# ScalarE's table loaded behind a copy of a constant, and the compressed attention of a decoder block in one stacked product for three

## The chip, the core and the metric

One core of a Trainium2 chip runs the whole kernel. The metric is the device time of one execution in microseconds (us); less is better. The engines are named as in the profile: PE is TensorE's matmul, PEld its weight load, DVE is VectorE, ACT is ScalarE, POOL is GpSimd, SP is SyncE, which here only issues DMAs.

## What is computed

One layer of a decoder trunk for 256 rows of 2048 columns, float32. The part that the change touches is the sparse attention with compressed keys and values:

```python
hn = rms_norm(h, ln_gain[l])
z = split_columns(hn @ w_in[l] + b_in[l])
y_a = rglru_branch(...) * silu(z['lru_gate'])
k_c = rms_norm(compress(z['nsa_k_cmp'], ...), nsa_k_gain[l])   # 15 compressed keys for each of 2 heads
v_c = compress(z['nsa_v_cmp'], cmp_pos[l, 1], cmp_w1[l, 1], cmp_w2[l, 1])
y_b = nsa_branch(q_b, k_c, v_c, k_s, v_s, k_w, v_w, g_b) * silu(z['nsa_gate'])
#   in it: o_c = p_c @ v_c, and out = g0 * o_c + g1 * o_s + g2 * o_w
y_c = fox_branch(...) * silu(z['fox_gate'])
merged = mg0 * (y_a @ w_branch[0]) + mg1 * (y_b @ w_branch[1]) + mg2 * (y_c @ w_branch[2])
h = h + merged @ w_out[l]
h = h + sigmoid(h @ w_ple_gate[l]) * rms_norm(p[l] @ w_ple[l], ple_gain[l])
```

`compress` is `silu(windows @ w1) @ w2` over 15 windows of 32 rows.

## The kernel before

Precision is kept by splitting each float32 operand into two float32r parts, `hi` (ACT copies it, rounding) and `lo` (DVE subtracts `hi` from the source). A product is then three matmuls, hi*hi, hi*lo, lo*hi, into the same PSUM bank (`mm3`).

The kernel is a stream of weights. `plan()` cuts all weight matrices into 385 pieces of at most 128 x 1024; each is loaded into one of four `raw` tiles by a DMA that SP issues (`issue`), split by ACT and DVE into `wh` and `wl` (`cut`, up to three pieces ahead, in a ring of four buffers each), and used by PE (`by_rows`, `by_cols`) into the PSUM banks `main0` to `main3`. Beside the stream runs the rest, as Python generators (`Side`): each step of a task is emitted between two pieces of the stream, in an order that a rough clock of the engines (`Clock`) decides when the program is built. On the chip each engine works through its own list in that order. The tasks use the PSUM banks `bank0` to `bank3`, and tiles of the pools `k1`, `k2`, `k4`, whose number in use `ROOMS` bounds; at most three tasks are under way.

Three places matter here.

- **The start** (`block_kernel`, "loads and constants"). ACT issues the DMAs of the small vectors `vec` and of the constants `cst`; SP issues by turns a tile of x (`xT`) and the first weights (`raw`). PE multiplies constants meanwhile (`WARM` = 8 products of 128 x 128 float32, each two passes in the trace). The first instruction of ACT with arithmetic is the split of x times its gain (`hn_first`, tile `hnh`); ahead of it stands ACT's table load. The first chunk is `cmp`, eight pieces of two 128-row tiles, 24 matmuls each.
- **`cmp_end`**: the hidden values `hid` of the compressed keys and values, their second product with `w2`, and the compressed values of each head as two tiles of 15 rows, `vch` and `vcl`.
- **`nsa_task(g, pr, t)`**, eight of them: two heads of a group and one row tile. It makes the scores, `soft` gives the probabilities `pc` (16 columns, compressed) and `p` (selected and window), DVE scales them with the gates, PE turns them (transposes against `ident`), and ACT and DVE split what comes out. The output is a sum in one bank: 6 matmuls (t = 0) or 12 (t = 1) of `pth`, `ptl` with the values `vv`, and then one `mm3` of 15 rows, `pch`, `pcl` with `vch`, `vcl`:

```python
        mm3(out, vch[:, g, :], vcl[:, g, :], pch[:NCMP].rearrange("p a q -> p (a q)"),
            pcl[:NCMP].rearrange("p a q -> p (a q)"), False, True)
```

Of the kernel before, what the change touches and what calls it, by code (L numbers as in the profile page):

```python
# [13 lines left out]
OP = mybir.AluOpType  # L14
# [14 lines left out]
HID = 256  # L29
KT = D // P  # L30
# [10 lines left out]
# The small vectors, one column of 128 rows each.  # L41
# [8 lines left out]
# Constants of the shapes alone.  # L50
# [9 lines left out]
# Columns of the input projection whose products come out with rows on partitions, by chunk.  # L60
# [15 lines left out]
def plan():  # L76
    """The order of the weights: pieces of products, with what each needs and starts."""
# [63 lines left out]
class Clock:  # L141
    """Estimates, in ns, of when each engine is through with what was emitted for it: an instruction
    starts once its engine is free and the last uses of its operands that matter to it are over."""
# [6 lines left out]
    def add(self, which, cost, out, ins, late=0.0):  # L150
# [3 lines left out]
        for ap, writes in regions:  # L154
            free = list(ap.ap)[1:]
            lo = ap.offset
            hi = lo + sum(s * (n - 1) for s, n in free)
            name = ap.tensor.name
            # Two engines take turns at a bank of PSUM, whatever they do there.
            bank = name.startswith(("bank", "main"))  # L160
            if bank:
                lo, hi = 0, 1 << 30
            spans.append((name, lo, hi, writes))
            for l, h, t, w, e in self.uses.get(name, ()):
                if (writes or w or bank and e != which) and l <= hi and lo <= h:
                    start = max(start, t + (0.0 if e == which else 60.0))
# [14 lines left out]
class Metered:  # L181
    """An engine whose work is added to the clock."""
# [37 lines left out]
class Side:  # L220
    """Work beside the stream of weights, cut into steps that are dealt out along it."""
# [17 lines left out]
    def tick(self, hurry=False):  # L239
        """One step of every task that is under way, as long as the engines keep up."""  # L240
# [17 lines left out]
    def take(self, n=1):  # L258
        """n banks that are through with what was last in them."""
# [11 lines left out]
    def settle(self):  # L271
        """Until a product that reads what was emitted so far needn't wait for it."""
# [5 lines left out]
    def room(self, **need):  # L278
        """Room for a task's tiles."""
# [14 lines left out]
def block_kernel(ctx: ExitStack, tc: tile.TileContext, io):  # L294
# [44 lines left out]
    def splits(*parts):  # L339
        """Each source (times a scale) as the exact sum of two float32r tensors."""  # L340
# [16 lines left out]
    # ------------------------------------------------------------------ the stream of weights  # L357
# [4 lines left out]
    def issue(h, k=0, nk=None):  # L362
        """Loads a half's rows of 128, or nk of them from the k-th."""
# [20 lines left out]
    def by_rows(h, x):  # L384
        """Rows on partitions: two main banks, one of each row tile, gather the chunk's products."""
# [14 lines left out]
    def by_cols(h, x):  # L400
        """Columns on partitions: the chunk's column tiles in halves of main banks."""
# [14 lines left out]
    def banks_of(h):  # L416
        """The main banks of by_cols, each with its (first column tile, number of them)."""
# [7 lines left out]
    # ------------------------------------------------------------------ loads and constants  # L425
# [7 lines left out]

    A.dma_start(vec, io["vec"])
    for i in range(4):
# [8 lines left out]
    # The causal mask of a tile, with none before and after.  # L444
# [9 lines left out]
    half_n = cp.tile([P, 8], F32, name="half_n")  # L454
    ones = cp.tile([P, P], F32, name="ones")
    V.memset(half_n, -0.5)
    V.memset(ones, 1.0)
    # Products of constants until the first weights are in: the array's clock rises with use.
# [3 lines left out]
    def rsqrt(out, ss, n):  # L462
        """out = (ss / n + EPS) ** -0.5"""
# [4 lines left out]
    def softplus(out, x, n):  # L468
        """out = max(x, 0) + log1p(exp(-|x|)), with log1p(u) = 2 atanh(u / (2 + u))"""
# [14 lines left out]
    def squares(x, acc, first):  # L484
        """acc += x^2, of two tiles"""
# [7 lines left out]
    def row_scales(name, acc):  # L493
        """(mean square of each of the 256 columns + EPS) ** -0.5, the same on all partitions."""
# [18 lines left out]
    # ------------------------------------------------------------------ operands kept on chip  # L513
# [9 lines left out]
    vch, vcl = (cp.tile([NCMP, 2, P], R32, name=n) for n in ("vch", "vcl"))  # L523
# [3 lines left out]
    def hn_first(i, ks=range(2)):  # L527
        """Two tiles of x times its gain, as operands; the rows' scales come later."""
# [9 lines left out]
    def hn_again(i):  # L538
        """The same with the rows' scales."""
# [14 lines left out]
    # ---- p @ w_ple, normed, with its gain halved for the last gate  # L554
# [28 lines left out]
    # ---- gates: half of z (1 + tanh(z / 2)) is z sigmoid(z)  # L583
# [11 lines left out]
    # ---- RG-LRU, two tiles of 128 channels at a time  # L595
    def lru_task(i):
# [43 lines left out]
        # 1 - a^2 = tanh(-log a) (1 + a^2)  # L640
# [12 lines left out]
    # ---- keys and values of the sparse attention  # L653
    def unscaled(banks, dst, name, k0):
        """A chunk of the products without the rows' scales."""
# [9 lines left out]
    def cmp_task(banks):  # L665
        """The windows of 32 rows, with their positions added: 15 columns for each row and head."""
# [19 lines left out]
    def cmp_end():  # L686
# [6 lines left out]
        # The products with both parts of each block, added and turned.  # L693
# [7 lines left out]
        V.tensor_tensor(hid, hp, sg, op=OP.mult)  # L701
        yield from side.settle()
        for q in range(2):
            T.matmul(banks[b][:30, 128:256], hid[:, q, :], w2[:, 0, q, :], start=q == 0, stop=q == 1)
        for g in range(2):
            for q in range(2):
                T.matmul(banks[b][:NCMP, 256 + g * P:256 + (g + 1) * P], hid[:, 2 + q, g * NCMP:(g + 1) * NCMP],
                         w2[:, 1, q, :], start=q == 0, stop=q == 1)
        yield True
        split(vch, vcl, banks[b][:NCMP, 256:512].rearrange("p (g d) -> p g d", g=2))  # L710
# [14 lines left out]
    def norm_rows(z, n, dst):  # L725
        """dst(t) = z's groups of 128 columns, each row of a group normed."""
# [15 lines left out]
    def kk_task(z):  # L742
        # Of each head: window keys of row tiles 1 and 0, compressed keys, selected keys of tiles 0 and 1.
# [21 lines left out]
    # ---- sparse attention of a pair of heads and one row tile  # L765
    def nsa_task(g, pr, t):
# [5 lines left out]
        yield from side.room(k1=2, k4=1)  # L772
# [9 lines left out]
        pc = sml([P, 2, 16], name="pc")  # L782
        p = mid([P, 2, 2, n * P], name="prob")

        def soft(a, sc):
            """exp(score - maximum) and their sums: compressed, selected, window."""
# [30 lines left out]
        for a in range(2):  # L817
            V.tensor_scalar(pc[:, a, :], pc[:, a, :], s[:, a, 0:1], None, op0=OP.mult)
# [16 lines left out]
        yield from side.room(k1=2)  # L835
        b, = yield from side.take()
        for a in range(2):
            T.transpose(banks[b][:16, 256 + a * P:256 + (a + 1) * P], pc[:, a, :], ident)
        yield True
        pch, pcl = one([16, 2, P], R32, name="pch"), one([16, 2, P], R32, name="pcl")  # L840
        split(pch, pcl, banks[b][:16, 256:512].rearrange("p (a q) -> p a q", a=2))
        yield from side.settle()
        out = banks[b][:, :S]
        for i in range(2 * n):
# [5 lines left out]
        mm3(out, vch[:, g, :], vcl[:, g, :], pch[:NCMP].rearrange("p a q -> p (a q)"),  # L850
            pcl[:NCMP].rearrange("p a q -> p (a q)"), False, True)
# [6 lines left out]
    # ---- forgetting attention  # L858
    def forget_task():
# [10 lines left out]
        # lf holds softplus(-f) = -log f: the running sum is minus the cumulative log forget gate.  # L870
# [10 lines left out]
    def fox_task(h):  # L881
# [42 lines left out]
        # Key tile 0 of both row tiles, then key tile 1 of the second.  # L924
# [17 lines left out]
    # ---- branch outputs as operands  # L942
# [24 lines left out]
    def split_turned(name, dst, src, j, scale=None):  # L967
        """Columns 512 j .. of src, turned and split into dst."""
# [15 lines left out]
    # ------------------------------------------------------------------ the ends of chunks  # L984
# [49 lines left out]
    def read_by(name, gen):  # L1034
        """A task that reads the chunk's main banks."""
# [30 lines left out]
    def proj_chunk(h, out):  # L1066
        """merged += projection (1 + tanh): twice the gated sum, halved when it is split."""
# [33 lines left out]
    def before(h):  # L1101
        """What the end of a chunk asks for, loaded while its products are formed."""
# [202 lines left out]
```

## Time and profile before

| | |
|---|---|
| timed runs | 1108.59, 1110.47, 1111.84 us; median 1110.47 |
| profiled execution | span 1108.5 us from its first to its last instruction; no other time of it is listed, and the shortest timed run is 0.1 us above this span |
| PE busy | 99% of the span, 6123 matmul passes |
| DVE, ACT, POOL busy | 65%, 53%, 5% |
| chain that ended last | PE 97% |
| DMA | 199 GB/s on average |

Busy shares count the time in which an instruction of the engine was under way; matmuls overlap, so the pace of PE is read from the start of one product to the start of the next. "Idle before" is the time in which an engine had nothing under way ahead of an instruction, with what ended it.

### The profile page before, as it was taken

Reading aid. Unit: us, or ns where it says so; the run is one execution under the profiler, and the core shown is the slowest. Engines: PE = TensorE matmul, PEld = TensorE weight load, DVE = VectorE, ACT = ScalarE, POOL = GpSimd, SP = SyncE. Lnnn points to the kernel's source line nnn. Section 1 sums busy time; section 2 is a strip of 40 time slices with the busy share of each in tenths; the row PEclk is TensorE's granted clock in tenths of the full one; section 3 lists DMA queues with packets and bytes.
Section 4 is the critical chain, followed back from the end, with each engine's and each line's share of the span. In section 5 each row is a group of like instructions: output and inputs, shape, how many; then the busy total and the mean of one; then the engine's idle time right before and its main releaser. Section 6 shows DMA issues by size and latency. Waiting matters only on the chain.

```text
span 1108.5 us, 16051 instructions
## 1 busy us (share of the span) xinstructions
PE 1098.8 (99%) x6123; PEld 957.4 (86%) x6123; DVE 725.9 (65%) x1108; ACT 588.2 (53%) x869; POOL 51.0 (5%) x70
## 2 busy tenths in 40 slices
PE   8999999999999999999999999999999999999998
PEld 8999998789988888888888888889888888888888
DVE  7679878877674765676776755554665565555554
ACT  7456786587654655454644544454554444444442
POOL 0100000010000000011010000000000100000000
PEclk9999999999999999999999999999999999999999
DMA  8656658756464554567557566766575775655773
GB/s 303 219 186 187 212 179 267 257 182 195 156 208 148 172 170 138 172 203 212 175 177 218 167 196 202 218 193 217 171 216 195 237 279 195 208 190 180 226 244 101
DMA packets 63293, 220.88 MB, mean 199 GB/s; under 512 B 7400, under 2 KB 8304, under 8 KB 63216
## 3 DMA queue, kind: packets, MB, share of 16 engines
q1 hardware_dynamic: 58176, 203.71, 55.6%
q0 software_dynamic: 4752, 15.76, 5.5%
q8 instruction: 48, 0.79, 0.3%
q10 hardware_dynamic: 288, 0.39, 0.1%
q14 instruction: 29, 0.24, 0.1%
HBM read 215.62 MB, written 4.20 MB: 198 GB/s over the span
## 4 chain that ended last, share of the span: by engine, by line
PE 97%; DMA 1%; DVE 1%; ACT 1%; issue 0%; DVEq 0%; ACTq 0%
PE main L191 90%; PE bank L191 7%; DMA raw<-in_w 1%; DVE wl L191 1%; ACT wh L191 0%; DMA k_xT<-in_xT 0%; ACT L191 0%; DVE k_fin L191 0%; DVE k_z L191 0%; ACT k_lru L191 0%; ACT k_hnh L191 0%; ACT k_fin L191 0%; DVEq L191 0%; ACTq L191 0%
## 5 line engine op out<-in xcount | busy, mean ns | idle before, releaser
L191 DVE TENSOR_TENSOR wl<-raw,wh 128x1024 fp32r<-128x1024 f32 (+3 forms) x385 | 463.8, 1211 | 320.2 <-ACT wh L191 319.1
L191 ACT ACTIVATE wh<-raw 128x1024 fp32r<-128x1024 f32 (+3 forms) x385 | 401.2, 1048 | 376.2 <-PE main L191 297.3
L191 PE MATMUL main<-wh,k_hnh 128*128 128x512 f32 (+1 forms) x736 | 285.0, 387 | 0.9 <-ACT wh L191 0.9
L191 PE MATMUL main<-wl,k_hnh 128*128 128x512 f32 (+1 forms) x736 | 281.3, 382 | 1.2 <-DVE wl L191 1.1
L191 PE MATMUL main<-wh,k_hnl 128*128 128x512 f32 (+1 forms) x736 | 281.0, 382 | 0.0
L191 PE MATMUL main<-k_hnh,wh 128*128 128x256 f32 x576 | 164.7, 286 | 1.5 <-ACT wh L191 1.5
L191 PE MATMUL main<-k_hnh,wl 128*128 128x256 f32 x576 | 164.1, 285 | 0.2 <-DVE wl L191 0.2
L191 PE MATMUL main<-k_hnl,wh 128*128 128x256 f32 x576 | 164.0, 285 | 0.0
L191 PEld LDWEIGHTS main<-wl,k_hnh 128*128 128x128 f32 x736 | 138.5, 188 | 26.7 <-DVE wl L191 2.6
L191 PEld LDWEIGHTS main<-wh,k_hnl 128*128 128x128 f32 x736 | 138.2, 188 | 26.7
L191 PEld LDWEIGHTS main<-wh,k_hnh 128*128 128x128 f32 x736 | 138.4, 188 | 26.3 <-ACT wh L191 1.2
L191 PEld LDWEIGHTS main<-k_hnh,wh 128*128 128x128 f32 x576 | 111.3, 193 | 2.0 <-ACT wh L191 1.8
L191 PEld LDWEIGHTS main<-k_hnh,wl 128*128 128x128 f32 x576 | 111.3, 193 | 0.5 <-DVE wl L191 0.4
L191 PEld LDWEIGHTS main<-k_hnl,wh 128*128 128x128 f32 x576 | 111.4, 193 | 0.1
L191 PE MATMUL main<-wh,k_yh 128*128 128x512 f32 x192 | 75.3, 392 | 0.0
L191 PE MATMUL main<-wh,k_yl 128*128 128x512 f32 x192 | 74.9, 390 | 0.0
L191 PE MATMUL main<-wl,k_yh 128*128 128x512 f32 x192 | 74.9, 390 | 0.0
L191 PE MATMUL main<-wh,k_hth 128*128 128x512 f32 (+1 forms) x160 | 55.7, 348 | 0.0
L191 PE MATMUL main<-wh,k_htl 128*128 128x512 f32 (+1 forms) x160 | 55.6, 347 | 0.0
L191 PE MATMUL main<-wl,k_hth 128*128 128x512 f32 (+1 forms) x160 | 55.5, 347 | 0.0
L191 PE MATMUL main<-wh,k_mth 128*128 128x512 f32 x128 | 50.7, 396 | 0.0
L191 PE MATMUL main<-wh,k_mtl 128*128 128x512 f32 x128 | 50.0, 391 | 0.0
(253 smaller groups left out, 1173.9 us busy)
## 6 DMA issues: line engine op xcount, KB each, us to landing
raw<-in_w SPq DMA_DIRECT2D x371, 512.0 KB, 4.1
bias<-in_b_in POOLq DMA_DIRECT2D x21, 256.0 KB, 4.3
raw<-in_w SPq DMA_DIRECT2D x8, 408.0 KB, 5.4
e_dram<-k_e POOLq DMA_DIRECT2D x4, 512.0 KB, 7.0
k_xc<-in_x POOLq DMA_DIRECT2D x4, 512.0 KB, 8.7
k_xT<-in_xT SPq DMA_DIRECT2D x7, 256.0 KB, 5.8
k_ec<-e_dram POOLq DMA_DIRECT2D x3, 512.0 KB, 7.8
out<-k_fin SPq DMA_DIRECT2D x6, 256.0 KB, 2.2
```

The costliest lines, as they stand in the source:

```text
L191: r = call(out, *args, **kw)
```

## The change

At the start, a copy of eight columns of a constant (`half_n`, set by DVE) is put on ACT right behind the DMA of `vec`, so that the table load stands ahead of this copy, and the DMA of `cst` behind it. PE gets 11 products of constants in place of 8. In `cmp_end` the hidden values of the compressed values are laid out three times, 32 columns apart, in a zeroed tile `hid3`, so that the second product gives 80 rows that hold the 15 values three times; `vc3` keeps them as hi, hi, lo. In `nsa_task` the compressed probabilities are laid out three times in a zeroed tile `pc3`, turned into 80 rows, and `pct` keeps them as hi, lo, hi. One matmul over 80 rows gives the sum of the three products. The tile `pc3` is taken with `qh` and `ql`, so that a task asks for three `k1` tiles at its start and one later, where it asked for two and two.

```diff
+NC3 = 80
...
-    vch, vcl = (cp.tile([NCMP, 2, P], R32, name=n) for n in ("vch", "vcl"))
+    vc3 = cp.tile([NC3, 2, P], R32, name="vc3")
...
+    half_n = cp.tile([P, 8], F32, name="half_n")
+    ones = cp.tile([P, P], F32, name="ones")
+    V.memset(half_n, -0.5)
+    V.memset(ones, 1.0)
     A.dma_start(vec, io["vec"])
+    A.activation(sml([P, 8], name="tbl"), half_n, AF.Copy)
...
     A.dma_start(cst, io["cst"])
...
 def cmp_end():
+        hid3 = two([P, 2, 2, 96], name="hid3")
+        G.memset(hid3, 0.0)
+        for i in range(3):
+            V.tensor_copy(hid3[:, :, :, 32 * i:32 * i + NCMP], hid[:, 2:, :].rearrange("p q (g i) -> p q g i", g=2))
...
-                T.matmul(banks[b][:NCMP, 256 + g * P:256 + (g + 1) * P], hid[:, 2 + q, g * NCMP:(g + 1) * NCMP],
+                T.matmul(banks[b][:NC3, 256 + g * P:256 + (g + 1) * P], hid3[:, q, g, :NC3],
                          w2[:, 1, q, :], start=q == 0, stop=q == 1)
-        split(vch, vcl, banks[b][:NCMP, 256:512].rearrange("p (g d) -> p g d", g=2))
+        v3 = banks[b][:NC3, 256:512].rearrange("p (g d) -> p g d", g=2)
+        A.activation(vc3, v3, AF.Copy)
+        V.tensor_tensor(vc3[64:], v3[64:], f(vc3[64:]), op=OP.subtract)
...
 def nsa_task(g, pr, t):
-        yield from side.room(k1=2, k4=1)
+        yield from side.room(k1=3, k4=1)
...
-        pc = sml([P, 2, 16], name="pc")
+        pc, pc3 = sml([P, 2, 16], name="pc"), one([P, 2, 96], name="pc3")
+        G.memset(pc3, 0.0)
...
-            V.tensor_scalar(pc[:, a, :], pc[:, a, :], s[:, a, 0:1], None, op0=OP.mult)
+            V.tensor_scalar(pc3[:, a, :].rearrange("p (i c) -> p i c", i=3)[:, :, :16],
+                            pc[:, a, None, :].to_broadcast([P, 3, 16]), s[:, a, 0:1], None, op0=OP.mult)
...
-        yield from side.room(k1=2)
+        yield from side.room(k1=1)
         b, = yield from side.take()
         for a in range(2):
-            T.transpose(banks[b][:16, 256 + a * P:256 + (a + 1) * P], pc[:, a, :], ident)
+            T.transpose(banks[b][:NC3, 256 + a * P:256 + (a + 1) * P], pc3[:, a, :NC3], ident)
         yield True
-        pch, pcl = one([16, 2, P], R32, name="pch"), one([16, 2, P], R32, name="pcl")
-        split(pch, pcl, banks[b][:16, 256:512].rearrange("p (a q) -> p a q", a=2))
+        pct = one([NC3, 2, P], R32, name="pct")
+        src = banks[b][:NC3, 256:512].rearrange("p (a q) -> p a q", a=2)
+        A.activation(pct, src, AF.Copy)
+        V.tensor_tensor(pct[32:64], src[32:64], f(pct[32:64]), op=OP.subtract)
...
-        mm3(out, vch[:, g, :], vcl[:, g, :], pch[:NCMP].rearrange("p a q -> p (a q)"),
-            pcl[:NCMP].rearrange("p a q -> p (a q)"), False, True)
+        T.matmul(out, vc3[:, g, :], pct.rearrange("p a q -> p (a q)"), start=False, stop=True)
...
-WARM = 8
+WARM = 11
```

The change also moves instructions, since the builder's clock and the rooms see other tasks. Three places are shown; L191 and L192 are the line of the same helper, through which all instructions go. On ACT, the first rows before:

```order
L191 DMA vec<-in_vec 128x184
L191 DMA cst<-in_cst 128x574
L191 ACT_TABLE_LOAD
L191 ACTIVATE k_hnh_125<-k_xT_91,vec 128x256
L191 ACTIVATE wh_142<-raw_97 128x512
```

and with the change:

```order
L192 DMA vec<-in_vec 128x184
L192 ACT_TABLE_LOAD
L192 ACTIVATE sp_tbl_100<-half_n 128x8
L192 DMA cst<-in_cst 128x574
L192 ACTIVATE k_hnh_130<-k_xT_91,vec 128x256
L192 ACTIVATE wh_146<-raw_103 128x512
```

The load stands ahead of the copy of the constant, and the DMA of `cst` has gone behind both.

On PE, the end of the first `nsa_task` before (`pth`, `ptl`, `pch`, `pcl` are the probabilities, `vv`, `vch`, `vcl` the values):

```order
L191 MATMUL bank_90<-k_pth_3583,k_vv_2106 128x256 x2
L191 MATMUL bank_90<-k_ptl_3584,k_vv_2106 128x256
L191 MATMUL bank_90<-k_pth_3583,k_vv_2106 128x256
L191 MATMUL bank_90<-k_pch_3739,vch 128x256
L191 MATMUL bank_90<-k_pcl_3740,vch 128x256
L191 MATMUL bank_90<-k_pch_3739,vcl 128x256
L191 MATMUL main_85<-wh_3709,k_hnh_125 128x512
```

and with the change:

```order
L192 MATMUL bank_90<-k_pth_3565,k_vv_2110 128x256 x2
L192 MATMUL bank_90<-k_ptl_3566,k_vv_2110 128x256
L192 MATMUL bank_90<-k_pth_3565,k_vv_2110 128x256
L192 MATMUL bank_90<-k_pct_3609,vc_142 128x256
L192 MATMUL main_83<-wh_3614,k_yh_3464 128x512
```

Three products have become one, and the task now ends one part of a chunk earlier, ahead of a product with `yh` rather than `hnh`.

On POOL, the rows from the second product of the compressed keys to the end of the eight tasks before (`bias` is the bias of the next chunk, loaded into a single buffer):

```order
L191 TENSOR_TENSOR sp_kcs_2767<-sp_kcs_2767,half_n 30x1
L191 DMA c_dram<-k_csum_2772 8x256
L191 TENSOR_TENSOR sp_nss_2878<-sp_nss_2878,half_n 128x8
L191 DMA bias_3477<-in_b_in 128x512
L191 DMA bias_3755<-in_b_in 128x512
L191 DMA bias_4124<-in_b_in 128x512
L191 DMA bias_4502<-in_b_in 128x512
```

and part of them with the change:

```order
L192 TENSOR_TENSOR sp_nss_2867<-sp_nss_2867,half_n 128x8
L192 MEMSET k_pc_455_3290 128x192
L192 MEMSET k_pc_460_3302 128x192
L192 DMA bias_3474<-in_b_in 128x512
L192 MEMSET k_pc_503_3586 128x192
L192 DMA bias_3793<-in_b_in 128x512
L192 MEMSET k_pc_555_3896 128x192
L192 MEMSET k_pc_565_3952 128x192
L192 DMA bias_4163<-in_b_in 128x512
```

The zeroing of `pc3` for each task stands on POOL between the DMAs of the biases.

## Rows read from the trace of the kernel before

**Rows 1.** The profile's page: the span, busy time of the engines, the clock granted to TensorE in 40 equal slices (tenths), and the shares of the chain that ended last.

```profile
span 1108.5 us, 16051 instructions
PE 1098.8 (99%) x6123; PEld 957.4 (86%) x6123; DVE 725.9 (65%) x1108; ACT 588.2 (53%) x869; POOL 51.0 (5%) x70
PEclk9999999999999999999999999999999999999999
PE 97%; DMA 1%; DVE 1%; ACT 1%; issue 0%; DVEq 0%; ACTq 0%
```

**Rows 2.** What PE waited for in the whole execution, the two longest in total: us in total, times, the longest.

```profile
PE main L191 <- ACT wh L191: 2.5, 2, 1.5
PE main L191 <- DVE wl L191: 1.4, 3, 0.7
```

**Rows 3.** Timeline of PE at the end of the first `nsa_task`, 335.7 to 337.9 us: start, duration (us), engine, operation, out<-in, shapes.

```profile
336.52 0.28 PE L191 MATMUL bank<-k_pth,k_vv 128*128 128x256 f32 x1
336.73 0.38 PE L191 MATMUL bank<-k_pch,vch 15*128 15x256 f32 x1
336.95 0.28 PE L191 MATMUL bank<-k_pcl,vch 15*128 15x256 f32 x1
337.07 0.27 PE L191 MATMUL bank<-k_pch,vcl 15*128 15x256 f32 x1
337.28 0.50 PE L191 MATMUL main<-wh,k_hnh 128*128 128x512 f32 x1
337.62 0.40 PE L191 MATMUL main<-wl,k_hnh 128*128 128x512 f32 x1
337.85 0.39 PE L191 MATMUL main<-wh,k_hnl 128*128 128x512 f32 x1
```

**Rows 4.** The group of the first of the three products: line, operands, shapes and count, then busy us and mean ns of one, and idle time before.

```profile
L191 PE MATMUL bank<-k_pch,vch 15*128 15x256 f32 x8 | 3.1, 382 | 0.0
```

**Rows 5.** Timeline of PE at the eight passes over 60 rows in `cmp_end`, same columns as rows 3.

```profile
228.46 0.39 PE L191 MATMUL main<-wh,k_hnl 128*128 128x512 f32 x1
228.78 1.07 PE L191 MATMUL bank<-cst,k_hs 60*128 60x30 f32 x8
229.78 0.50 PE L191 MATMUL main<-wh,k_hnh 128*128 128x512 f32 x1
230.12 0.40 PE L191 MATMUL main<-wl,k_hnh 128*128 128x512 f32 x1
```

**Rows 6.** Timeline of PE at two transposes to 16 columns, and at two to 128 columns.

```profile
330.26 0.38 PE L191 MATMUL bank<-cst,sp_pc 128*16 128x128 f32 x2
...
330.71 0.40 PE L191 MATMUL main<-wl,k_hnh 128*128 128x512 f32 x1
...
372.89 0.38 PE L191 MATMUL bank<-cst,k_qn 128*128 128x128 f32 x2
...
373.34 0.39 PE L191 MATMUL main<-wl,k_hnh 128*128 128x512 f32 x1
```

**Rows 7.** Timeline of ACT at the start, with the idle time ahead and what ended it.

```profile
4.01 1.28 ACT L191 ACT_TABLE_LOAD   x1 [4.01 <-DMA k_xT<-in_xT]
5.31 0.51 ACT L191 ACTIVATE k_hnh<-k_xT,vec 128x256 fp32r<-128x256 f32 x1
9.28 1.06 ACT L191 ACTIVATE wh<-raw 128x1024 fp32r<-128x1024 f32 x1 [0.34 <-DMA raw<-in_w]
```

**Rows 8.** Timeline of PE and DVE at the start (the constants' products, the first piece's, and the weights of the second piece).

```profile
1.09 3.76 PE L191 MATMUL bank<-ones 128*128 128x128 f32 x16 [1.09 <-DVE ones L191]
6.39 0.39 PE L191 MATMUL main<-k_hnh,wh 128*128 128x256 f32 x1 [1.54 <-ACT wh L191]
10.36 1.23 DVE L191 TENSOR_TENSOR wl<-raw,wh 128x1024 fp32r<-128x1024 f32 x1 [0.91 <-ACT wh L191]
11.41 0.34 PE L191 MATMUL main<-k_hnl,wh 128*128 128x256 f32 x1
11.64 0.39 PE L191 MATMUL main<-k_hnh,wl 128*128 128x256 f32 x1
```

**Rows 9.** Busy time by stretch of the start: start:end, length, then busy us (and instructions) of PE, PEld, DVE, ACT, POOL, TensorE's granted clock, DMA share, GB/s.

```profile
4.70:8.10 3.40, 1.64 (x11) 1.29 (x11) 2.17 (x4) 2.65 (x6) 0.00 (x0) 1.00 1.02 370
8.10:11.50 3.40, 3.40 (x18) 3.40 (x17) 2.02 (x3) 2.96 (x6) 0.00 (x0) 0.50 1.04 399
11.50:14.90 3.40, 3.40 (x29) 3.29 (x29) 3.15 (x7) 3.40 (x6) 0.00 (x0) 1.00 1.03 406
```

**Rows 10.** The same view of the stretch in which the eight tasks stand, with the columns of rows 9.

```profile
285.00:465.00 180.00, 180.00 (x921) 151.26 (x920) 115.28 (x277) 98.69 (x208) 2.15 (x4) 1.00 0.49 164
```

**Rows 11.** Who waited for whom from 225 to 465 us: us in total, times, the longest.

```profile
DVE wl L191 <- ACT wh L191: 63.1, 44, 3.7
ACT wh L191 <- PE main L191: 41.4, 27, 2.6
```

**Rows 12.** Groups on POOL and DVE that are nearest to the new memsets and copies: count, busy us, mean ns (or, in the last, least, median and greatest ns).

```profile
L191 POOL TENSOR_TENSOR sp_nss<-sp_nss,half_n 128x8 f32<-128x8 f32 x7 | 15.7, 2244 | 235.6 <-DVE sp_nss L191 179.8 <-ACT wh L191 40.8 <-DVE sp_fs L191 14.9
L1298 POOL MEMSET const-float32-1.0<- 128x1 f32 x1 | 0.1, 95 | 0.0
L191 DVE MEMSET ones<- 128x128 f32 x1 | 0.2, 165 | 0.0
L191 DVE TENSOR_SCALAR sp_pc<-sp_pc,sp_sm x16: 225/232/235, 294.5 to 446.4; 128x16 f32<-128x16 f32 x16
```

More of the change, by code (lines that the diff above doesn't have):

```diff
@@ L453, in block_kernel @@
     c_dram = dp.tile([8, S], F32, name="c_dram")
[L454 to L457, printed above, removed]
     for _ in range(WARM):
```

## The prediction

> **What bounds the kernel now.** First the page: PE is busy 99% of the span, its clock is granted in full in nearly every slice, and 97% of the chain that ended last is PE [rows 1]. DVE and ACT, the next two, are busy 65% and 53%. A busy share alone could hide slow matmuls, so I looked next at what PE waited for: 2.5 us for ACT and 1.4 us for DVE are the two longest totals of 1108 us [rows 2]. So PE works through its list almost without a stop, and the time is the sum of the paces of its products. That gives the rule for the rest: what shortens PE's list by a microsecond is worth a microsecond, and what another engine gains or loses is worth nothing as long as PE does not wait for it. Then I read the two places of the change in the timeline: the end of a sparse attention task, and the first 15 us.
>
> **The stacked product.** In the timeline a product of 256 columns is followed by the next after 0.12 us (336.95 to 337.07), one of 512 columns after 0.23 us (337.62 to 337.85). At the three products of 15 rows the pace is broken [rows 3]: from the last `pth` product at 336.52 it takes 0.21, 0.22, 0.12 and 0.21 us to the next starts, and 0.34 us from the first `main` product to the second. Together 336.52 to 337.62 is 1.10 us, where the `pth` product and one `main` product would take 0.12 + 0.23 = 0.35 us. So the three cost 0.75 us: 3 x 0.12 for their columns, and 0.39 us in four breaks of about 0.1 us, two where the rows go from 128 to 15 and two where they go back. There are eight such places [rows 4].
>
> What one product over 80 rows costs is not in the trace; nothing in it has between 60 and 128 rows. The bounds are these. If it runs like the products of 128 rows around it, it costs 0.12 us, and a task saves 0.63 us, eight tasks 5.0 us. If the breaks stay, it costs 0.12 + 0.39 = 0.51 us, a task saves 0.24 us, and eight save 1.9 us. The row with most rows below 128 is the group over 60: it has the same breaks, 0.32 in place of 0.23 us going in (228.46 to 228.78) and 0.34 in place of 0.23 us coming out (229.78 to 230.12) [rows 5]. So the break does not grow or shrink with the rows, from 15 to 60: it looks like a change of the array's arrangement that a product makes or doesn't. By count, 80 is nearer to 60 than to 128; but 15 and 60 rows both fit into half of the array and 80 do not, and I take that as the dividing line: 5.0 us, chance about three in four.
>
> The Trainium skill, page "TensorEngine Tiling (Array Packing)", sections Tiling Modes and Key Properties, says that the array runs with 128, 64 or 32 rows to a tile, and that a change of mode drains the engine. By that rule 80 rows need the same mode as 128, the breaks go, and the sum would be 5.0 us. Against it, the same skill's page "TensorE: Matmul & The Clock Gate", section Why this matters for your kernels, says that a single product over 32 rows takes the same time as one over 128; by that alone only two products of 0.12 us fall away per task, 1.9 us in all. The trace speaks against the second as it stands, since 15 rows cost 0.25 us a product with the breaks and 0.12 us without.
>
> **What is added beside it.** The transposes of the probabilities now give 80 columns for 16. Two to 16 columns take 330.26 to 330.71, two to 128 columns 372.89 to 373.34 [rows 6]: 0.45 us both, to the second `main` product. So 80 cost the same: 0, with 8 x 0.02 us as the bound. In `cmp_end` eight passes over 128 rows give 80 columns for 15: 0 by the same rows. ACT's split keeps its number of columns, and so does DVE's subtraction. DVE gets 16 scalings of 48 columns for 16 columns, each 0.23 us before [rows 12], at most about 0.05 us more each, under 1 us in all, and three small copies of some 0.25 us once. DVE was busy 115 of 180 us in the stretch of the tasks [rows 10], and ACT waited 41.4 us there for PE to give weight buffers back [rows 11]. That idle time is the cover, and I cost these at nothing.
>
> POOL gets nine memsets. POOL was busy 2 of the 180 us [rows 10]. A memset of one column takes 0.095 us there, one of 128 columns on DVE 0.165 us; the farthest row, a power of 8 columns on POOL, takes 2.2 us [rows 12]. I take 0.3 us for 192 columns, the memsets being nearer than a power. Each stands in POOL's queue between the DMAs of the biases, and DVE's scaling waits for it; behind that scaling, on DVE, stand the next `wl` pieces, and for those PE waits. The cover is the store of up to three cut pieces, each 12 products of 0.23 us = 2.8 us of PE, so about 8 us. At 0.3 us nothing comes through.
>
> The order of the tasks moves too, but PE's products in it are the same, and the pace of a `main` product does not depend on where a group of 128 rows is put in. I cost it at nothing; without the cover just named, each piece cut late would cost its lateness.
>
> **The start.** ACT sits until the first tile of x lands at 4.01, loads the table for 1.28 us, and starts the first split at 5.31 [rows 7]. PE is through with the constants at 4.85, sits 1.54 us, and starts at 6.39 [rows 8]. With the load done earlier the split can start at about 4.0 and the first product up to 1.28 us earlier, at 5.1 or, if the weights land after x, later. The constants took 3.76 us for 8, 0.47 us each [rows 8], so 11 end at 1.09 + 11 x 0.47 = 6.3 at the latest, and PE starts the real work between 0.1 and 1.28 us earlier. Does that reach the end? No, by the next row: the second piece of weights lands at 9.28, after an idle ACT [rows 7], with the DMA engines full (share 1.02 to 1.04) [rows 9]. ACT and DVE cut it to 11.59, and PE starts on `wl` at 11.64 [rows 8]. The DMAs ahead of that piece are the same in bytes; `cst` only moves among them. So PE arrives earlier at 11.64 and waits there: gain 0, bounded above by the whole load, 1.28 us.
>
> It can cost instead. After the idle 1.54 us the granted clock was 0.50 from 8.1 to 11.5, the lower level of 1.2 GHz, and full again after 3.4 us of work without a pause [rows 9]. At the half clock PE spread its first 26 products up to 11.41, and lost nothing, since the next had to wait anyway. With the change PE has these 26 done by about 9 at 0.12 us each, and then waits some 2.5 us until 11.6. If a stretch at half clock follows this pause as it followed the other, it falls on products that nothing covers: 18 products against 29 in an equal stretch at the full clock [rows 9], 11 x 0.12 = 1.3 us. Between 0 and 1.3 us I take +0.7 us, the middle, since nothing in the rows says where such a stretch would begin.
>
> **The sum.** Against the profiled execution's span, which lies 0.1 us below the shortest run: 1108.5 - 5.0 + 0.7 = 1104.2 us. The median of the runs shown lies 2.0 us above that span, so as a median: 1110.5 - 4.3 = **1106.2 us**.
>
> **Rivals.**
> 1. *The breaks stay with 80 rows.* For it: 80 is nearer to 60 than to 128. Then 1110.5 - 1.9 + 0.7 = 1109.3 us. This is also the case in which the change does not do what its three-for-one promises beyond two products less, and the same time follows from the second page named above.
> 2. *The start gains as well.* If the second piece lands earlier because `cst` no longer stands ahead of the first weights, the load's 1.28 us come through: 1110.5 - 5.0 - 1.3 = 1104.2 us. Against it stands the full DMA share.
> 3. *Slower: the memset of `pc3` holds DVE.* From about 8 us beyond its due time, the store of cut pieces is empty, and every further microsecond is paid in each of eight tasks. For a net loss of 3.3 us it has to cost 3.3 + 4.3 = 7.6 us, about 1 us past the cover per task: 1114 us. Only a memset of 9 us would do it, four times the longest POOL row.
>
> **How the numbers follow.** Chances: forecast 0.70, rival 1 0.18, rival 2 0.08, rival 3 0.04. About 0.3%, 3.3 us, is what a measurement of this kernel can tell from no change; the three runs before already spread over 3.2 us. Faster by more means under 1107.1 us. The forecast's own range is 1103.5 to 1108.0 (start 0 to +1.3, and the spread of a median by about 1 us); about 0.8 of it lies under 1107.1, so 0.56. Rival 2 adds 0.07, rival 1 0.02: faster 0.65. Slower is rival 3, 0.04. The rest, 0.31, is within 0.3%. For eight in ten I reach up to rival 1, 1110.0, and down to 1103.0, rival 2 less the spread.
>
> **What would show it.** Right: at the ends of the tasks one product over 80 rows starts 0.12 us after the last `pth`, and the next `main` 0.12 us after it. Wrong: starts 0.2 us apart there. At the start: the table load ends before x lands, the first product starts at 5.3 to 6.3, PE waits again until about 11.6, and the granted clock may be half somewhere after that; the first `wl` of the second piece well before 11.6 would speak for rival 2. PE waits from 285 to 465 us, of which there were none, with DVE's scaling into `pc3` behind a POOL memset, would speak for rival 3.

## The result, and the profile after

The changed kernel takes 1104.10 us (median of five runs, 1103.58 to 1106.32) where the kernel before takes 1110.41 (five runs, 1108.59 to 1111.84): a ratio of 0.9948 with an interval of 0.9936 to 0.9959, 0.52% or 5.8 us less (the ratio is of the means; the medians lie 6.3 us apart). The profiled execution has a span of 1101.6 us and a time of its own of 1103.76. The forecast was 1106.2 us, 2.1 us too high; the measured median lies inside the forecast's own range of 1103.5 to 1108.0.

The page of the changed kernel, its span, busy times, granted clock and chain, answers to [rows 1]:

```profile
span 1101.6 us, 16062 instructions
PE 1092.9 (99%) x6113; PEld 954.5 (87%) x6113; DVE 728.5 (66%) x1111; ACT 587.4 (53%) x870; POOL 52.3 (5%) x79
PEclk9999999999999999999999999999999999999999
PE 96%; DVE 1%; ACT 1%; DMA 1%; issue 0%; SPq 0%; DVEq 0%; ACTq 0%
```

PE is busy 5.9 us less and is still the bound. It has ten passes fewer: 16 less at the eight tasks, 6 more from three more constants in two passes each. The waits of PE over the execution (us in total, times, the longest) answer to [rows 2]:

```profile
PE main L192 <- DVE wl L192: 2.4, 5, 0.8
PE main L192 <- ACT wh L192: 1.1, 2, 0.7
```

Together they are 3.5 us, as against 3.9 before, so the waits are not where the 5.8 us went. The timeline of PE at the end of a `nsa_task` shows where (start, duration, engine, operation, shapes; the place of [rows 3]):

```profile
320.88 0.28 PE L192 MATMUL bank<-k_ptl,k_vv 128*128 128x256 f32 x1
321.00 0.28 PE L192 MATMUL bank<-k_pth,k_vv 128*128 128x256 f32 x1
321.12 0.28 PE L192 MATMUL bank<-k_pct,vc 80*128 80x256 f32 x1
321.24 0.40 PE L192 MATMUL main<-wh,k_yh 128*128 128x512 f32 x1
321.48 0.40 PE L192 MATMUL main<-wl,k_yh 128*128 128x512 f32 x1
```

All starts go on at the pace of the products over 128 rows, 0.12 us after a product of 256 columns and 0.24 after one of 512. From the last `pth` to the second `main` product it is 0.48 us; in [rows 3] the same way took 1.10. So 0.62 us per task, 5.0 us for eight. (Before, all eight tasks take 1.09 or 1.10; with the change five take 0.47 or 0.48, and the other three are followed by transposes in place of a `main` product, also without a break.)

The transposes that now give 80 columns take 0.46 us to the second `main` product, as did those to 16 and 128 columns (0.45, [rows 6]):

```profile
310.64 0.38 PE L192 MATMUL bank<-cst,k_pc 128*80 128x128 f32 x2
310.78 0.47 PE L192 MATMUL main<-wh,k_hnh 128*128 128x512 f32 x1
311.10 0.39 PE L192 MATMUL main<-wl,k_hnh 128*128 128x512 f32 x1
```

The memsets of `pc3` on POOL (count, then busy us and mean ns of one, then idle time before):

```profile
L192 POOL MEMSET k_pc<- 128x192 f32 x8 | 2.1, 263 | 88.1 <-PE bank L192 44.5 <-DVE k_gn L192 38.4 <-ACT wh L192 5.1
```

They take 0.26 us each, and POOL sits idle 88.1 us ahead of them, most of it ended by PE, DVE or ACT, without harm: PE has no wait listed from 285 to 465 us.

The start is the second place. The timelines of ACT's queue, ACT, PE and DVE, beside [rows 7] and [rows 8]:

```profile
1.24 0.39 ACTq L192 DMA_DIRECT2D cst<-in_cst  x1
1.18 1.28 ACT L192 ACT_TABLE_LOAD   x1 [1.18 <-PEq L1312]
2.47 0.21 ACT L192 ACTIVATE sp_tbl<-half_n 128x8 f32<-128x8 f32 x1
4.82 0.63 ACT L192 ACTIVATE wh<-raw 128x512 fp32r<-128x512 f32 x1 [0.87 <-DMA raw<-in_w]
9.32 1.06 ACT L192 ACTIVATE wh<-raw 128x1024 fp32r<-128x1024 f32 x1 [0.43 <-DMA raw<-in_w]
1.09 4.07 PE L192 MATMUL bank<-ones 128*128 128x128 f32 x22 [1.09 <-DVE ones L192]
5.50 0.39 PE L192 MATMUL main<-k_hnh,wh 128*128 128x256 f32 x1 [0.34 <-ACT wh L192]
11.69 0.39 PE L192 MATMUL main<-k_hnh,wl 128*128 128x256 f32 x1 [0.76 <-DVE wl L192]
```

The table is loaded by 2.46 us and the first product starts at 5.50 instead of 6.39. The second piece lands at 9.32 as before (9.28), and PE reaches its `wl` at 11.69, as before (11.64). The granted clock (the next to last figures are clock and DMA share; columns of [rows 9]) stays full, though PE has far less to do between 8.1 and 11.5 us:

```profile
8.10:11.50 3.40, 1.95 (x12) 1.54 (x12) 2.06 (x4) 2.65 (x6) 0.00 (x0) 1.00 1.02 389
11.50:14.90 3.40, 3.21 (x26) 3.21 (x27) 2.98 (x7) 3.40 (x6) 0.00 (x0) 1.00 1.03 410
```

### The profile page after: what moved, and what is told of

Same layout as the page of the kernel before. It is cut to its first block, busy times and chain, and to the rows that moved or that the text cites. A ratio compares the mean times of both kernels' runs of the same rounds, so it can differ in the third digit from the quotient of the medians.

```text
span 1101.6 us, 16062 instructions
## 1 busy us (share of the span) xinstructions
PE 1092.9 (99%) x6113; PEld 954.5 (87%) x6113; DVE 728.5 (66%) x1111; ACT 587.4 (53%) x870; POOL 52.3 (5%) x79
## 3 DMA queue, kind: packets, MB, share of 16 engines
q1 hardware_dynamic: 58176, 203.71, 55.5%
## 4 chain that ended last, share of the span: by engine, by line
PE 96%; DVE 1%; ACT 1%; DMA 1%; issue 0%; SPq 0%; DVEq 0%; ACTq 0%
PE main L192 90%; PE bank L192 6%; DMA raw<-in_w 1%; DVE wl L192 1%; ACT wh L192 1%; ACT k_lru L192 0%; ACT L192 0%; SPq L192 0%; DVE k_lru L192 0%; DVE sp_nss L192 0%; DVE k_fin L192 0%; DVE k_z L192 0%; ACT k_fin L192 0%; DVEq L192 0%; ACTq L192 0%
## 5 line engine op out<-in xcount | busy, mean ns | idle before, releaser
L192 DVE TENSOR_TENSOR wl<-raw,wh 128x1024 fp32r<-128x1024 f32 (+3 forms) x385 | 463.2, 1211 | 312.2 <-ACT wh L192 309.5
L192 ACT ACTIVATE wh<-raw 128x1024 fp32r<-128x1024 f32 (+3 forms) x385 | 401.1, 1048 | 374.8 <-PE main L192 288.0
L192 PE MATMUL main<-wh,k_hnh 128*128 128x512 f32 (+1 forms) x736 | 284.0, 386 | 0.0
L192 PE MATMUL main<-wl,k_hnh 128*128 128x512 f32 (+1 forms) x736 | 280.7, 381 | 1.2 <-DVE wl L192 1.2
L192 PE MATMUL main<-wh,k_hnl 128*128 128x512 f32 (+1 forms) x736 | 280.7, 381 | 0.0
L192 PE MATMUL main<-k_hnh,wh 128*128 128x256 f32 x576 | 163.8, 284 | 1.1 <-ACT wh L192 1.1
L192 PE MATMUL main<-k_hnh,wl 128*128 128x256 f32 x576 | 163.3, 283 | 1.2 <-DVE wl L192 1.2
L192 PE MATMUL main<-k_hnl,wh 128*128 128x256 f32 x576 | 163.0, 283 | 0.0
L192 PEld LDWEIGHTS main<-wh,k_hnl 128*128 128x128 f32 x736 | 138.2, 188 | 27.0
L192 PEld LDWEIGHTS main<-wl,k_hnh 128*128 128x128 f32 x736 | 138.4, 188 | 26.4 <-DVE wl L192 2.2
L192 PEld LDWEIGHTS main<-wh,k_hnh 128*128 128x128 f32 x736 | 138.3, 188 | 24.5 <-ACT wh L192 0.2
L192 PEld LDWEIGHTS main<-k_hnh,wl 128*128 128x128 f32 x576 | 110.5, 192 | 1.8 <-DVE wl L192 1.8
L192 PEld LDWEIGHTS main<-k_hnh,wh 128*128 128x128 f32 x576 | 110.5, 192 | 1.7 <-ACT wh L192 1.5
L192 PEld LDWEIGHTS main<-k_hnl,wh 128*128 128x128 f32 x576 | 110.5, 192 | 0.1
L192 PE MATMUL main<-wh,k_yh 128*128 128x512 f32 x192 | 75.2, 392 | 0.0
L192 PE MATMUL main<-wh,k_yl 128*128 128x512 f32 x192 | 74.8, 390 | 0.0
L192 PE MATMUL main<-wl,k_yh 128*128 128x512 f32 x192 | 74.8, 389 | 0.0
L192 PE MATMUL main<-wh,k_hth 128*128 128x512 f32 (+1 forms) x160 | 55.7, 348 | 0.0
L192 PE MATMUL main<-wh,k_htl 128*128 128x512 f32 (+1 forms) x160 | 55.5, 347 | 0.0
L192 PE MATMUL main<-wl,k_hth 128*128 128x512 f32 (+1 forms) x160 | 55.5, 347 | 0.0
L192 PE MATMUL main<-wh,k_mth 128*128 128x512 f32 x128 | 50.6, 395 | 0.0
L192 PE MATMUL main<-wh,k_mtl 128*128 128x512 f32 x128 | 49.9, 390 | 0.0
```

What stands on the lines that cost most here:

```text
L192: r = call(out, *args, **kw)
```

## The experiments

The theory: the breaks of the 15-row products go because 80 rows do not fit into half of the array, −5.0 us, and the start is worth about nothing or a little loss. The rivals: only the two products less count (−1.9 us); or the start gives a part of the gain. Ratios are to the kernel before, run again beside each group of experiments (1110.0, 1109.9 and 1109.8 us).

**The kernel before, again**, without an edit, to see what no change looks like.

> The kernel before, once more, as a control for the trace. Between 171 and 226 us of the two traces in hand the order of all instructions is the same, and yet the changed kernel is 2.0 us quicker there. If that is a difference of executions, the trace of this one lies anywhere between the two in that stretch, and not always at the slow end. If the change causes it (the theory that the start reaches that far), this trace shows the slow end again, 57.8 us from the first transposes of zn at 170.7 to the first pass over 60 rows.

Measured 1110.26 us, ratio 1.0003 (0.9994 to 1.0012), span 1109.5. In its trace x lands earlier, the table load starts at 3.35 us and the first product at 5.73, nearly as early as in the changed kernel. PE is on the second piece's `wl` at 12.04. So between two executions of one kernel the arrival there differs by 0.4 us, more than the change moved it.

**The stacked product alone**: the changed kernel without the copy, and with 8 constants.

```diff
-    A.activation(sml([P, 8], name="tbl"), half_n, AF.Copy)
-WARM = 11
+WARM = 8
```

> The stacked attention alone, with the old start (no copy of a constant, 8 constant products). Theory A, the stack is all: -5.0 us against before by the sum (8 x 0.63), and the same time as the changed kernel. Theory B, the start brings the microsecond that the sum does not explain: -4.9 us here, and the changed kernel 1 us quicker than this.

Measured 1105.08 us, ratio 0.9955 (0.9943 to 0.9967): −4.9 us.

**The start alone**: the kernel before with the copy, the two memsets ahead of it and 11 constants; run twice.

```diff
+    V.memset(half_n, -0.5)
+    V.memset(ones, 1.0)
     A.dma_start(vec, io["vec"])
+    A.activation(sml([P, 8], name="tbl"), half_n, AF.Copy)
-WARM = 8
+WARM = 11
```

> The new start alone (copy of the constant for the table load, 11 constant products), attention as before. Theory A: 0 against before, within 0.7 us, since PE still resumes at about 11.65 us on the second piece's wl. Theory B: -1 us. The rival from the prediction's sum, a stretch at half clock that nothing covers: up to +1.3 us.

> The new start alone, once more, for the same question: under 2.5 us of waits between 100 and 228 us and -0.9 us against before if the start causes both; waits up to 4.3 us and a time within 0.5 us of before if the first result was chance.

Measured 1109.04 us, 0.9992 (0.9984 to 1.0000), and 1108.96 us, 0.9990 (0.9981 to 0.9999): −0.9 us twice, each with an interval that reaches 1.0000 or almost. With the −4.9 us of the stack that is the 5.8 us of the whole. A small gain, where I had taken a small loss.

**Which half of the start: the copy alone, the constants alone** (the kernel before with one of the two edits).

> The kernel before with the copy of the constant alone (8 constant products). The start alone was 0.9 us quicker with both parts. If the table load is what counts: about -0.9 us here. If the first 15 us gain nothing, as PE resumes on the second piece at 11.5 to 12 us either way, and the gain lies in the loads of weights from 160 to 226 us by chance of the executions: 0, and waits there of 1.3 to 4.3 us, with no regard to the start.

> The kernel before with 11 constant products alone. If the constant products are what counts in the start (no stretch at half clock): about -0.9 us. If the load is: 0, or a little slower, since 11 products end at 6.3 us at the latest, still ahead of the 6.39 us at which the first product started. By the theory of chance from 160 to 226 us: 0.

The copy alone: 1109.77 us, 1.0001 (0.9993 to 1.0010). The 11 constants alone: 1108.57 us, 0.9991 (0.9982 to 1.0000). The load's 1.28 us are worth nothing. ACT and PE in the trace with the copy alone show why:

```profile
1.19 1.28 ACT L191 ACT_TABLE_LOAD   x1 [1.19 <-PEq L1299]
9.43 1.06 ACT L191 ACTIVATE wh<-raw 128x1024 fp32r<-128x1024 f32 x1 [0.38 <-DMA raw<-in_w]
11.80 0.39 PE L191 MATMUL main<-k_hnh,wl 128*128 128x256 f32 x1 [0.75 <-DVE wl L191]
```

The load is out of the way, and the second piece still lands at 9.4 us.

**The changed kernel with 8 constants, and the changed kernel again.** The first asks whether the constants are worth the same in the other surroundings.

```diff
-WARM = 11
+WARM = 8
```

> The changed kernel with 8 constant products in place of 11. The copy alone moved nothing and 11 products alone gave about -1 us on the kernel before. If that microsecond is real and belongs to the products, this kernel is 1 us slower than the changed one, 1105.1 us, like the stack alone. If it is chance, they agree.

> The changed kernel once more. The five traces with the whole new start waited 1.3 to 2.4 us for weights between 100 and 228 us, the five others 3.0 to 4.3 us, with the same instructions there. If the start causes it, this trace waits under 2.5 us again; if it differs by execution, it may wait anything from 1.3 to 4.3 us.

Measured 1105.39 us, 0.9964 (0.9951 to 0.9976), and 1104.54 us, 0.9949 (0.9936 to 0.9961): 0.85 us for the constants, the same size, though with five runs each the two intervals overlap. The trace of the changed kernel, run again, also has what the prediction allowed for, a stretch of half clock on products that nothing covers (columns of [rows 9]):

```profile
11.00:12.27 1.27, 0.51 (x4) 0.41 (x4) 1.27 (x3) 1.18 (x2) 0.00 (x0) 1.00 1.02 410
12.27:15.68 3.41, 3.41 (x18) 3.41 (x18) 3.17 (x5) 3.41 (x8) 0.00 (x0) 0.50 1.04 409
15.68:19.09 3.41, 3.41 (x30) 3.41 (x30) 3.41 (x7) 3.41 (x6) 0.00 (x0) 1.00 1.03 399
```

18 products against 30 in an equal stretch. It came after a pause like that of the first trace, in which the clock stayed full. So it does happen, but not in every execution.

**`cst` behind the second piece**: in the changed kernel the DMA of `cst` is moved to ACT's place behind the split of the second piece (issued at 9.50 us), so that its bytes are out of the way of the weights.

```diff
-    A.dma_start(cst, io["cst"])
...
+    A.dma_start(cst, io["cst"])
     issued, ready = 4, 2
```

> The changed kernel with the DMA of the constants issued on ACT behind the split of the second piece, so that its 287 KB no longer stand among the first loads. If the arrival of the second piece is what sets the start, as read from the full DMA share, that piece lands earlier by the 287 KB at some 370 GB/s, 0.8 us, PE resumes at about 10.9 instead of 11.7 us, and the whole is 0.8 us quicker than the changed kernel. If the start is set by something else, 0.

Measured 1104.59 us, 0.9952 (0.9940 to 0.9964), no gain. ACT and PE at the second piece:

```profile
9.50 1.06 ACT L192 ACTIVATE wh<-raw 128x1024 fp32r<-128x1024 f32 x1 [0.36 <-DMA raw<-in_w]
11.87 0.39 PE L192 MATMUL main<-k_hnh,wl 128*128 128x256 f32 x1 [0.76 <-DVE wl L192]
```

The first piece is split earlier, at 4.08 us against 4.82, but with 287 KB less ahead of it the second piece does not land earlier. This refutes rival 2, and also a part of my own reasoning: full DMA engines do not explain the landing by the bytes ahead. From 4.7 to 8.1 us the engines were as busy and moved less (columns of [rows 9], the changed kernel first):

```profile
4.70:8.10 3.40, 2.76 (x19) 2.12 (x17) 1.78 (x3) 1.89 (x4) 0.00 (x0) 1.00 0.94 331
```

```profile
4.70:8.10 3.40, 3.02 (x21) 2.80 (x20) 1.51 (x3) 1.14 (x3) 0.00 (x0) 1.00 0.97 278
```

**64 rows for 80**: the last product reads only the first two parts of the stack and leaves the third out of the result.

```diff
-        T.matmul(out, vc3[:, g, :], pct.rearrange("p a q -> p (a q)"), start=False, stop=True)
+        T.matmul(out, vc3[:64, g, :], pct[:64].rearrange("p a q -> p (a q)"), start=False, stop=True)
```

> The changed kernel with its last product of a task over the first 64 of the 80 rows; it leaves out the part hi of the probabilities times lo of the values. If the breaks come when a product's rows fit into half of the array (the dividing line of the prediction), the four breaks of about 0.1 us are back at all eight places: a task's end takes 0.39 us more, the whole 3.1 us more than the changed kernel, some 1107.3 us. If 80 rows were fast only because there is one product instead of three, 64 rows cost the same as 80: 0.

Measured 1107.03 us, 0.9977 (0.9968 to 0.9986), 2.9 us more than the changed kernel, with a product of the same number and the same columns. PE at the place shown above:

```profile
321.27 0.28 PE L192 MATMUL bank<-k_pth,k_vv 128*128 128x256 f32 x1
321.48 0.38 PE L192 MATMUL bank<-k_pct,vc 64*128 64x256 f32 x1
321.79 0.50 PE L192 MATMUL main<-wh,k_yh 128*128 128x512 f32 x1
322.12 0.39 PE L192 MATMUL main<-wl,k_yh 128*128 128x512 f32 x1
```

From the last `pth` to the second `main` it is 0.85 us against 0.48: the breaks are back, 0.37 us per task (0.31 to 0.33 in the three tasks that transposes follow), 2.8 us for eight. 64 rows have them, 80 have not.

**The product over 80 rows three times**: one could say that the number of products matters and not their rows. Here each task issues the stacked product three times, and so adds the compressed part three times over.

```diff
-        T.matmul(out, vc3[:, g, :], pct.rearrange("p a q -> p (a q)"), start=False, stop=True)
+        for r in range(3):
+            T.matmul(out, vc3[:, g, :], pct.rearrange("p a q -> p (a q)"), start=False, stop=r == 2)
```

> The changed kernel with its product over 80 rows issued three times (it adds the same part three times). Priced by the prediction's terms, two more products of 0.12 us at eight places: +1.9 us against the changed kernel, some 1106.1 us, and no breaks; then 3.1 of the 5.0 us come from the breaks and 1.9 from the two products. If each product on rows below 128 costs 0.25 us, as the three of 15 did with their breaks: +4 us.

Measured 1106.36 us, 0.9969 (0.9957 to 0.9981). PE:

```profile
321.51 0.28 PE L192 MATMUL bank<-k_pth,k_vv 128*128 128x256 f32 x1
321.63 0.52 PE L192 MATMUL bank<-k_pct,vc 80*128 80x256 f32 x3
321.99 0.40 PE L192 MATMUL main<-wh,k_yh 128*128 128x512 f32 x1
322.23 0.40 PE L192 MATMUL main<-wl,k_yh 128*128 128x512 f32 x1
```

Three products of 80 rows take 0.36 us without a break, where three of 15 took 0.75. It costs 0.24 us more per task than one product, 1.9 us for eight (1.8 and 2.3 by the medians of the changed kernel's two sets of runs). So of the 5.0 us some 1.9 come from two products less and 3.1 from the breaks.

**A fifth `raw` tile**: where the traces still show PE waiting (below), ACT waits for weights to land. The changed kernel with one more load buffer:

```diff
-RAW, LOADS, AHEAD = 4, 5, 3
+RAW, LOADS, AHEAD = 5, 6, 3
```

> The changed kernel with five raw tiles and six loads ahead in place of four and five. The only waits of PE that are left after the start, 1.3 to 2.4 us between 170 and 216 us, end when weights land. If they come from loads that are issued too late for want of a tile, most of them go: -1 to -2 us. If the DMA engines' rate sets them (their share was 0.74 to 0.88 there), little changes: 0 to -0.5 us.

Measured 1101.16 us (1100.97 to 1101.33), 0.9922 (0.9908 to 0.9935), 2.9 us less than the changed kernel, more than expected, and the fastest of all. ACT's waits for the loads over the whole execution, the changed kernel first:

```profile
ACT wh L192 <- DMA raw<-in_w: 42.2, 32, 4.0
```

```profile
ACT wh L192 <- DMA raw<-in_w: 6.4, 12, 2.2
```

From 100 to 228 us no PE wait is left, and the runs spread over 0.4 us in place of 2.7.

## Why the prediction was right, and where it was not

**What bounds the kernel: right.** PE's list got shorter by 5.0 us at the tasks, and the time fell by it. What was put on DVE, ACT and POOL came through nowhere in that stretch.

**The stacked product: right, in mechanism and size.** The step that chose between −5.0 and −1.9 us was a reading of 15 and 60 rows against half of the array. 64 rows with the breaks and 80 without them put the line between the two (no run has a number of rows in between), and the stack alone measures −4.9 us. Rival 1 is refuted. The rule of the Trainium skill, page "TensorEngine Tiling (Array Packing)", sections Tiling Modes and Key Properties, by which a tile has 128, 64 or 32 rows and a change of mode drains the engine, agrees with both, if 80 rows run in the mode of 128. The price of a change stands only in the rows, 0.37 us for going in and coming out. By the Trainium skill's page "TensorE: Matmul & The Clock Gate", section Why this matters for your kernels, one product over 32 rows takes the same time as one over 128; that gave −1.9 us and leaves out this price.

**Transposes, scalings, memsets: right at 0.** 0.46 against 0.45 us; POOL's memset 0.26 us against the estimate of 0.3; DVE is busy 2.6 us more over the execution, and PE has no wait listed at the tasks. Rival 3 did not come.

**The table load: right at 0.** The copy alone measures nothing, although the load itself was moved fully ahead. The reason given was only half right. That the second piece sets the time holds in each trace; that it is late because the DMA engines are full with the bytes ahead does not, since 287 KB less did not move it, and 278 GB/s in place of 331 went with the same share. What sets its landing stays open. The order of the instructions also misled: `cst` stands behind load and copy in ACT's program, but its DMA was issued at 1.24 us, while the load still ran to 2.46.

**The half clock: this is the step that failed.** I took +0.7 us for the start: a gain of 0 from load and constants, and half the price of an uncovered stretch. The runs show −0.9. The stretch on uncovered products exists (18 products against 30, shown above), and where it came, PE reached its first product that reads `zn` at 172.0 us in place of 170.1 to 170.5, so it cost about what it was priced at (1.3 us) or a little more. But only one trace of nine with 11 constants has it. I had inferred a half-clock stretch from a pause of PE in a single execution; the next traces had the pause with the clock full. One detail of that step was also wrong: the 25th and 26th product cannot be done by about 9 us, since they read the second piece's `wh`; they started at 10.43 and 10.65.

Nor is there more of it with 11 constants. The three traces whose record has a half-clock stretch within the work (the kernel before, the stack alone, the changed kernel again) have a mean granted clock of 0.998, the others 0.999 or 1.000; and of all runs 52 of 98 with 8 constants have 0.998 or less, and 6 of 70 with 11. The mean does not say where the stretch lies. In the stack alone the record has it not at the start but behind a wait of PE of 1.74 us (a row of PE's timeline, then the stretch in the columns of [rows 9]). That trace also shows that the record is not complete: from 6.84 to 9.83 us its products start 0.21 us apart, nearly half the pace, while the clock's row says 1.00.

```profile
172.11 0.39 PE L192 MATMUL main<-wh,k_hnh 128*128 128x272 f32 x1 [1.74 <-ACT wh L192]
174.10:177.50 3.40, 3.40 (x17) 3.40 (x16) 3.32 (x6) 2.97 (x6) 1.07 (x2) 0.51 0.86 280
```

These stretches are not shown to be the 0.9 us. Among the runs of the old product with a mean clock of 1.000, those with 8 constants (30 runs) average 1109.8 us and those with 11 (21 runs) 1109.0: nearly the same gap. The traces put the difference elsewhere. PE is on the second piece's `wl` at 11.1 to 12.0 us with 8 constants and at 11.4 to 11.9 with 11, no difference, and on the first product that reads `zn` at 169.8 to 170.7 and, but for the trace named above, 170.1 to 170.5. But from there to the 60-row products with `hs` (about 228 us), where ACT waits for loads, it took 58.0 to 59.1 us in five traces with 8 constants, and 55.5 to 57.8 in eight with 11 (53.8 with the fifth `raw` tile). The waits of PE that are listed from 100 to 228 us sum to 2.1 to 3.2 us with 8 constants and to 0.7 to 2.1 with 11.

One thing there parts all fourteen traces. The queue q8, which the page lists as `instruction`, moves 48 packets of 16 KB for the 12,246 instructions of PE and PEld, one for some 256, so I take them for PE's code (an estimate). With 8 constants one of them starts at 167.8 to 169.1 us, 2.4 to 4.3 us after a weight load was issued; that load takes 5.5 to 6.4 us to land. With 11 the packet starts 0.7 to 1.2 us before that load is issued, and the load takes 4.3 to 4.6. Packets, and loads with their time to landing, from 165.2 to 169.2 us, in the kernel before and then in the changed kernel, which has no packet of q8 there:

```profile
q8 instruction: 1, 0.02, 1.5%
raw<-in_w SPq DMA_DIRECT2D x3, 408.0 KB, 5.6
```

```profile
raw<-in_w SPq DMA_DIRECT2D x3, 408.0 KB, 4.6
```

PE then waits for the split of this piece, 0.9 to 1.7 us in each of the five traces with 8 constants, and in one of the nine with 11 (0.4 us). In the kernel before:

```profile
171.86 0.39 PE L191 MATMUL main<-wh,k_hnh 128*128 128x272 f32 x1 [0.93 <-ACT wh L191]
```

Of the 16 signals of that load's landing the last comes 1.2 to 2.0 us behind the fifteenth with 8 constants and at most 0.3 us with 11, as if one of the 16 DMA engines had the code to move as well. So the likely cause is that three products more at the start shift PE's code against the weights. This is read from traces and not shown by a run: none moves the packet alone, six passes more take PE only 0.7 us at 0.12 us each while the packet moves by 3 to 5 us, and whether all of the 0.9 us comes from it stays open.

**The sum.** Of the 2.1 us between forecast and result, 1.6 are the start's term, +0.7 for −0.9; the rest lies within the spread of the runs. One reading of the times was wrong without harm: I took the span to lie 0.1 us under the execution's own time. In the later runs of the kernel before the time is 1.8 us over the span (1110.27 for 1108.5), so the profiled execution was an ordinary one and not the fastest.

## What to carry to other kernels

Where PE is the bound, look in its timeline for starts that are further apart than their columns say: a few products over 64 rows or fewer between products over 128 cost here twice, going in and coming out, and stacking them over 80 rows paid more by these breaks (3.1 us) than by the products saved (1.9 us). Work that an engine does earlier at the start is worth nothing while a later load sets the time; look for the last arrival first. When an edit changes a stretch that it does not touch, look at the DMA queues there, PE's code among them. After such a change read again who waits: one more load buffer gave more than the whole start.

## What the runs showed of the hardware

- A product over 64 rows between products over 128 costs 0.37 us in breaks, about what three over 15 rows did (0.39 us), and one over 80 rows has none.
- A DMA issue on ACT's queue does not wait for the table load or the copy ahead of it: issued at 1.24 us, with the load running from 1.18 to 2.46.
- The first ACTIVATE behind a table load started 0.01 us after its end (2.46 to 2.47).
- The pauses of PE between 8.1 and 11.5 us, 1.95 us busy of 3.4, were followed by full clock in one execution of the changed kernel and by 3.41 us at half clock in another.
- A 16 KB packet of the queue that carries instructions, in the middle of a 408 KB load of weights, went with 5.5 to 6.4 us to landing in place of 4.3 to 4.6, in five traces against nine.
